# Low parts of the plain feed-forward weights by accumulating DMA, and the embeddings' projection kept in HBM during the feed-forward

## The chip, the cores and the metric

The kernel runs on one core of a Trainium2 chip. The time is the device time of one execution in microseconds, the median of three runs. The engines are TensorE (PE; its weight loads are shown as PEld), VectorE (DVE), ScalarE (ACT), GpSimd (POOL) and SyncE (SP). Each takes its instructions in the order of its own queue. SP only issues DMAs here; POOL issues others and computes a few small things.

## The reference

One layer of a hybrid encoder on 512 tokens of width 1024, in float32. Only the last two of its three parts matter here:

```python
x = x + jnp.concatenate([a, r], axis=-1) @ w_o[l]          # attention and recurrence, before
h = rms_norm(x, g_ffn[l])
x = x + (jax.nn.silu(h @ w_gate[l]) * (h @ w_up[l])) @ w_down[l]
gate = jax.nn.sigmoid(rms_norm(x, g_ple[l]) @ w_ple_gate[l])
x = x + gate * (p[l].astype(x.dtype) @ w_ple_proj[l])
```

`w_gate` and `w_up` have 1024 rows and 2816 columns, 22 tiles of 128 columns; `p @ w_ple_proj` is the projection of the embeddings, 1024 features by 512 tokens, eight tiles of 128 x 512.

## The kernel before

All activations lie with the features on the 128 partitions and the 512 tokens along the row. To keep precision at TensorE's fast float32 format, each operand is split in two: a rounded high part, and a low part that is the rest. A product is three matmuls (`mm3`, lines 141 to 144): high times high, high times low, low times high. `split` (lines 132 to 139) makes the parts: ScalarE copies the operand into the rounding format, VectorE subtracts.

A second way to make a low part is there already for other weights (lines 154 to 157, 1160 to 1170): the high part is scaled by -1 into the low tile by ScalarE, and a DMA issued by POOL adds the same weights from HBM onto it (`accum_op=ALU.add`).

The feed-forward works on 22 pairs (a tile of `w_gate` and the same tile of `w_up`), in six parts of 4, 4, 4, 4, 3 and 3. After each part, eight products with `w_down` (names `dn`) add the part to the residual `xT`. The pairs of part 0 are plain (`pair_plain`, line 1036): `halves` (line 1019) loads the weight in two halves of 512 columns (tiles `raw`, `whi`, `wlo`), and 24 matmuls make one 128 x 512 result (`ff`). The result is multiplied by the token scale `bc2`. That scale comes from `token_rstd` (line 179) after the second plain tile: sums by TensorE (`ss`), VectorE, a power of -1/2 by POOL (`rs_tok`), eight small VectorE instructions (`dgh`, `dgl`), and two matmuls (`bc`, lines 195 and 196) that spread it over the partitions. TensorE's order puts these two matmuls behind the third plain tile.

The pairs of the other parts use seven half-size products in place of eight (`pair_seven`, line 1096): weights A11, A21, A22, A12 are loaded raw (line 1102, tiles `A`), VectorE makes sums of them (`S`, line 1112), each of the seven operands is split, and meets sums of the activations, which `block_sums` (line 1074) makes once, beside the plain pairs. These products are named `p`.

The embeddings' projection is made before the feed-forward, at the end of the mixer (lines 944 to 955): its eight results are copied by ScalarE to tiles `ppo`, and stay in SBUF until the last stage (lines 1232 to 1250), where each multiplies the gate.

Tiles of 128 x 512 come from a list of places, `A` (class `Slots`): `get` takes the first free place, `put` puts it at the end. A place is given out in program order, but the instruction that writes it waits on the chip until the last reader of the tile before has finished. A longer list of free places means that a place has lain longer when it comes around again. The order on each engine is made by a scheduler that works from a timeline of its own, so a change in places changes the order too.

Of the kernel before, what the change touches and what calls it, by code (L numbers as in the profile page):

```python
# [8 lines left out]
F32 = mybir.dt.float32  # L9
F32R = mybir.dt.float32r  # L10
I32 = mybir.dt.int32
AF = mybir.ActivationFunctionType
ALU = mybir.AluOpType
AX = mybir.AxisListType

P = 128
S = 512
NT = S // P
KT = 8
# [98 lines left out]
def layer_kernel(ctx: ExitStack, tc: tile.TileContext, io, out):  # L118
    nc = tc.nc
    act, dve, pool, pe, sp = nc.scalar, nc.vector, nc.gpsimd, nc.tensor, nc.sync  # L120

    cpool = ctx.enter_context(tc.tile_pool(name="cpool", bufs=1))
    small = ctx.enter_context(tc.tile_pool(name="small", bufs=4))
    spool = ctx.enter_context(tc.tile_pool(name="spool", bufs=1))
    ppool = ctx.enter_context(tc.tile_pool(name="ppool", bufs=1, space=bass.MemoryType.PSUM))
    mixer = ExitStack()
    wpool = mixer.enter_context(tc.tile_pool(name="wpool", bufs=WB))
    A = Slots(spool, SLOTS, "u")
# [3 lines left out]
    def split(hi, lo, src, scale=None, eng=dve):  # L132

        if scale is None:
            act.activation(hi, src, AF.Copy)  # L135
            eng.tensor_tensor(lo, src, hi, ALU.subtract)  # L136
        else:
            act.activation(hi, src, AF.Copy, scale=scale)
            dve.scalar_tensor_tensor(lo, src, scale, hi, ALU.mult, ALU.subtract)
# [24 lines left out]
    def cut(hl, a, b):  # L164
        return hl[0][:, a:b], hl[1][:, a:b]

    def ts(j):
        return slice(j * P, (j + 1) * P)

    def rsqrt_mean(o, ss, n):  # L170

        w = ss.shape[-1]
        v = small.tile([P, 8], F32, tag="rs_v", name="rs_v")
        dve.tensor_scalar(v[:, :w], ss, 1.0 / n, EPS, ALU.mult, ALU.add)
        pool.tensor_tensor(o, v[:, :w], mhalf[:, :w], ALU.pow)
# [3 lines left out]
    def token_rstd(sq, keep=None):  # L179


        p1 = B.get("ss")
        for j in range(NT):
            e = pe.matmul(p1[:, j : j + 1], lhsT=sq[:, ts(j)], rhs=ones[:, :1], start=True, stop=True)
        rs = (keep or small).tile([P, NT], F32, tag="rs_tok", name="rs_tok")
        rsqrt_mean(rs, p1[:, :NT], 1024.0)
        B.put(p1)

        dh, dl = A.get("dgh", F32R), A.get("dgl", F32R)
        for j in range(NT):  # L190
            dve.tensor_scalar(dh[:, ts(j)], ident, rs[:, j : j + 1], None, ALU.mult)
            dve.scalar_tensor_tensor(dl[:, ts(j)], ident, rs[:, j : j + 1], dh[:, ts(j)], ALU.mult, ALU.subtract)
        marks.append(e.ins)
        p2 = B.get("bc")
        pe.matmul(p2, lhsT=onesr, rhs=dh, start=True, stop=False)
        marks.append(pe.matmul(p2, lhsT=onesr, rhs=dl, start=False, stop=True).ins)
        bc = A.get("rsbc")
        act.copy(bc, p2)
        A.put(dh, dl)
        B.put(p2)  # L200
        return rs, bc
# [34 lines left out]
    t = B.get("warm")  # L236
# [365 lines left out]
    def wnext():  # L602
        while wlist and len(ahead) < AHEAD:
            nd[0] += 1
            ahead.append(weights(*wlist.popleft(), by_dma=nd[0] > LO_DVE))
        return ahead.popleft()
# [14 lines left out]
    def w_in_tokens(evacuate):  # L621

        for half in range(2):
            ws = [wnext(), wnext()]
            for jp in range(2):
                o = [BD.get("wt0"), BD.get("wt1")]
                for c in range(2):
                    for k in range(4 * c, 4 * c + 4):
                        a = (k % 4) * 256
                        for i in range(2):  # L630
                            j = 2 * jp + i
                            mm3(o[i][:, :256], cut(hT[k], j * P, j * P + P), cut(ws[c], a, a + 256), k == 0, k == KT - 1)
                        if k % 2:
                            yield 1.3
                for i in range(2):
                    evacuate(2 * jp + i, slice(half * 256, half * 256 + 256), o[i][:, :256])
                BD.put(*o)

    def gates(heads):

        zs = {}
        for h in heads:
            for d in range(2):
                z = []
                yield from w_in_tile(z)
                zs[h, d] = z[0]
        for h in heads:
            z = []
            yield from w_in_tile(z)
            q[h] = z[0]  # L650

        later.append(gate_steps(heads, zs))
# [3 lines left out]
    def spread(stream):  # L656

        for y in stream:
            yield y
            if later and next(later[0], None) is None:  # L660
                later.popleft()
# [35 lines left out]
    def output_gates():  # L697

        zs = []
        for h in range(H):  # L700
            yield from w_in_tile(zs)
        t = [A.get("sg") for h in range(H)]
        together([lambda h=h: act.activation(t[h], zs[h], AF.Sigmoid) for h in reversed(range(H))], exp_ln)
        for h in range(H):
            dve.scalar_tensor_tensor(zs[h], zs[h], vec[:, V_HGO + h : V_HGO + h + 1], t[h], ALU.mult, ALU.mult)
        A.put(*t)
        gg.extend(zs)
# [202 lines left out]
    def load_embeddings():  # L910
        for k in range(2):
            t = A.get("pin")
            sp.dma_start(t, io["pT"][k])
            hl = (A.get("ph", F32R), A.get("pl", F32R))
            split(hl[0], hl[1], t)
            A.put(t)
            pT.append(hl)

    def dense_stream():
        for what in ORDER:  # L920
            if what == "v":
                yield from spread(w_in_tokens(value_out))
                done.add("value")
            elif what == "g":
                yield from spread(output_gates())
            elif what == "p":
                load_embeddings()
            else:
                yield from spread(gates(what))
        done.add("gate")  # L930
        while later:
            if next(later[0], None) is None:
                later.popleft()
        for hl in hT:
            A.put(*hl)
        A.put(bc1)
        for m in range(KT):
            xT[m] = A.get(f"x{m}")
            sp.dma_start(xT[m], io["xT"][m])
        yield lambda: "attention" in done  # L940
        yield from w_o_half(0, aT, BD)
        for h in range(H):
            A.put(*aT[h])
        for c in range(2):
            w = wnext()
            for i in range(4):
                o = BD.get("pp")
                for k in range(2):
                    a = (i * 2 + k) * P
                    mm3(o, cut(w, a, a + P), pT[k], k == 0, k == 1)  # L950
                t = A.get("ppo")
                act.copy(t, o)
                BD.put(o)
                pp.append(t)
                yield 1.3
        for hl in pT:
            A.put(*hl)

    pp = []
# [56 lines left out]

    A.join(Slots(ctx.enter_context(tc.tile_pool(name="fpool", bufs=1)), SLOTS2, "f"), 12)

    def halves(src):

        ws = []
        for i in range(2):
            raw, hi, lo = A.get("raw"), A.get("whi", F32R), A.get("wlo", F32R)
            sp.dma_start(raw, src[:, i * 512 : i * 512 + 512])
            split(hi, lo, raw)
            A.put(raw)
            ws.append((hi, lo))
        return ws

    def part_of(ws, k):  # L1030
        return cut(ws[k // 4], k % 4 * P, k % 4 * P + P)

    bc2 = None
    tiles_done = 0

    def pair_plain(f):

        nonlocal bc2, tiles_done
        zz = []
        for name in ("w_gate", "w_up"):  # L1040
            w = halves(io[name][f])
            o = B.get("ff")
            with ExitStack() as behind:

                if tiles_done > 1:
                    behind.enter_context(tc.issue_after(marks[-4 + min(tiles_done, 3)]))
                for k in range(KT):
                    mm3(o, part_of(w, k), h2[k], k == 0, k == KT - 1)
            A.put(*w[0], *w[1])
            tiles_done += 1  # L1050
            if bc2 is None:
                bc2 = token_rstd(sq2)[1]
                A.put(sq2)
            z = A.get("z")
            dve.tensor_tensor(z, o, bc2, ALU.mult)
            B.put(o)
            zz.append(z)
        hl = (A.get("ah", F32R), A.get("al", F32R))
        act.activation(zz[0], zz[0], AF.Silu)
        dve.tensor_tensor(zz[0], zz[0], zz[1], ALU.mult)  # L1060
        split(hl[0], hl[1], zz[0])
        A.put(*zz)
        return hl
# [126 lines left out]
    f = 0  # L1190
# [38 lines left out]
        next_down()  # L1229


    rs3, bc3 = token_rstd(sq3)
    for m in range(KT):
        w = halves(io["w_pg"][m])
# [92 lines left out]
```

## Time and profile before

| | |
|---|---|
| median of three runs | 702.74 us (701.41 to 702.83) |
| the profiled execution | 700.41 us, of which the span of the trace is 698.6 |
| TensorE busy | 686.4 us (98%) |
| VectorE, ScalarE, POOL busy | 509.5, 383.2, 111.1 us (73, 55, 16%) |
| feed-forward | from 295 to 648 us: plain pairs to 348, seven-product pairs among the `dn` products after that; then the last stage |
| HBM read, written | 88.33 MB, 2.10 MB |

Times in rows are microseconds from the span's start. A row of the timeline is one instruction (or several merged, with their count behind the x): start, duration, engine, line, operation, the tiles it writes and reads, and in brackets how long the engine stood idle before it and what ended that. A busy TensorE is not TensorE at its peak: ends of matmuls are modelled, and the distance between two starts says more.

### The profile page before, as it was taken

Reading aid. Unit: us, or ns where it says so; the run is one execution under the profiler, and the core shown is the slowest. Engines: PE = TensorE matmul, PEld = TensorE weight load, DVE = VectorE, ACT = ScalarE, POOL = GpSimd, SP = SyncE. Lnnn points to the kernel's source line nnn. Section 1 sums busy time; section 2 is a strip of 40 time slices with the busy share of each in tenths; the row PEclk is TensorE's granted clock in tenths of the full one; section 3 lists DMA queues with packets and bytes.
Section 4 is the critical chain, followed back from the end, with each engine's and each line's share of the span. In section 5 each row is a group of like instructions: output and inputs, shape, how many; then the busy total and the mean of one; then the engine's idle time right before and its main releaser. Section 6 shows DMA issues by size and latency. Waiting matters only on the chain.

```text
span 698.6 us, 11350 instructions
## 1 busy us (share of the span) xinstructions
PE 686.4 (98%) x4170; PEld 604.2 (86%) x4170; DVE 509.5 (73%) x1031; ACT 383.2 (55%) x808; POOL 111.1 (16%) x144
## 2 busy tenths in 40 slices
PE   9999999899999999999989999999999999999997
PEld 8888887699878888878788999999999999998886
DVE  6944489797987943679987977877677578768663
ACT  7857795686645645535544554445544545546421
POOL 6233421101212222010111100001100110100000
PEclk9999999999999999999999999999999999999999
DMA  7575555543657657322456456345655664563111
GB/s 241 164 171 136 124 145 97 119 86 84 157 123 208 156 138 189 90 66 61 147 129 163 115 145 178 92 115 145 166 130 130 158 138 123 123 179 112 55 60 61
DMA packets 44264, 91.18 MB, mean 131 GB/s; under 512 B 5424, under 2 KB 11568, under 8 KB 44208
## 3 DMA queue, kind: packets, MB, share of 16 engines
q0 software_dynamic: 14976, 41.43, 28.8%
q1 hardware_dynamic: 29232, 49.02, 22.3%
q8 instruction: 33, 0.54, 0.3%
q14 instruction: 23, 0.19, 0.1%
HBM read 88.33 MB, written 2.10 MB: 129 GB/s over the span
## 4 chain that ended last, share of the span: by engine, by line
PE 86%; issue 8%; DMA 2%; ACT 2%; POOL 1%; DVE 1%; SPq 0%; POOLq 0%; ACTq 0%
PE p L144 8%; PE p L143 8%; PE p L142 8%; PE dn L143 5%; PE dn L144 5%; PE dn L142 5%; PE wi L143 4%; PE wi L142 4%; PE wi L144 4%; PE pg L144 2%; PE pg L142 2%; PE pg L143 2%; PE wo L142 2%; PE wo L144 2%; PE wo L143 2%
## 5 line engine op out<-in xcount | busy, mean ns | idle before, releaser
L142 PE MATMUL p<-bh,whi 128*128 128x256 f32 x432 | 122.3, 284 | 2.4 <-ACT whi L135 2.3
L143 PE MATMUL p<-bl,whi 128*128 128x256 f32 x432 | 121.8, 283 | 0.0
L144 PE MATMUL p<-bh,wlo 128*128 128x256 f32 x432 | 121.3, 283 | 0.0
L142 PEld LDWEIGHTS p<-bh,whi 128*128 128x128 f32 x432 | 82.7, 192 | 3.3 <-ACT whi L135 3.2
L143 PEld LDWEIGHTS p<-bl,whi 128*128 128x128 f32 x432 | 82.8, 192 | 0.1
L144 PEld LDWEIGHTS p<-bh,wlo 128*128 128x128 f32 x432 | 82.5, 192 | 0.1
L143 PE MATMUL dn<-al,whi 128*128 128x512 f32 x176 | 68.7, 390 | 0.0
L144 PE MATMUL dn<-ah,wlo 128*128 128x512 f32 x176 | 68.5, 389 | 0.0
L142 PE MATMUL dn<-ah,whi 128*128 128x512 f32 x176 | 67.7, 390 | 0.0
L1170 POOL DMA_DIRECT2D wlo<-in_w_d x32 | 27.4, 877 | 202.4 <-ACT wlo L1169 160.5
L1112 DVE TENSOR_TENSOR S<-A,A 128x512 f32<-128x512 f32 x36 | 24.4, 689 | 40.0 <-DMA A<-in_w_up 19.5
L135 ACT ACTIVATE whi<-A 128x512 fp32r<-128x512 f32 x54 | 33.6, 626 | 35.0 <-DMA A<-in_w_gate 22.8
L142 PE MATMUL wi<-hh,whi 128*128 128x512 f32 x128 | 51.2, 400 | 0.0
L144 PE MATMUL wi<-hh,wlo 128*128 128x512 f32 x128 | 50.9, 397 | 0.0
L143 PE MATMUL wi<-hl,whi 128*128 128x512 f32 x128 | 50.5, 394 | 0.0
L135 ACT ACTIVATE whi<-S 128x512 fp32r<-128x512 f32 x72 | 42.6, 623 | 10.3 <-DVE S L1112 9.0
L156 ACT ACTIVATE wlo<-whi 128x1024 fp32r<-128x1024 f32 x28 | 29.7, 1060 | 33.4 <-DMA whi<-in_w_hf 12.0
L136 DVE TENSOR_TENSOR wlo<-S,whi 128x512 fp32r<-128x512 f32 x72 | 46.3, 681 | 1.0 <-ACT whi L135 1.0
L135 ACT ACTIVATE whi<-raw 128x512 fp32r<-128x512 f32 (+2 forms) x42 | 25.5, 625 | 31.6 <-DMA raw<-in_w_up 9.7
L136 DVE TENSOR_TENSOR wlo<-A,whi 128x512 fp32r<-128x512 f32 x54 | 36.8, 682 | 3.1 <-ACT whi L135 3.1
L144 PEld LDWEIGHTS dn<-ah,wlo 128*128 128x128 f32 x176 | 33.1, 188 | 6.9
L142 PEld LDWEIGHTS dn<-ah,whi 128*128 128x128 f32 x176 | 33.0, 188 | 6.4
(342 smaller groups left out, 1840.6 us busy)
## 6 DMA issues: line engine op xcount, KB each, us to landing
A<-in_w_gate SPq DMA_DIRECT2D x36, 256.0 KB, 4.4
A<-in_w_up SPq DMA_DIRECT2D x36, 256.0 KB, 3.8
wlo<-in_w_d POOLq DMA_DIRECT2D x32, 256.0 KB, 5.3
whi<-in_w_hf POOLq DMA_DIRECT2D x14, 512.0 KB, 4.6
wlo<-in_w_hf POOLq DMA_DIRECT2D x14, 512.0 KB, 5.7
raw<-in_w_d SPq DMA_DIRECT2D x24, 256.0 KB, 2.8
x<-in_xT SPq DMA_DIRECT2D x16, 256.0 KB, 4.4
raw<-in_w_pg SPq DMA_DIRECT2D x16, 256.0 KB, 3.5
```

The costliest lines, as they stand in the source:

```text
L135: act.activation(hi, src, AF.Copy)
L136: eng.tensor_tensor(lo, src, hi, ALU.subtract)
L142: pe.matmul(o, lhsT=l[0], rhs=r[0], start=start, stop=False)
L143: pe.matmul(o, lhsT=l[0], rhs=r[1], start=False, stop=False)
L144: pe.matmul(o, lhsT=l[1], rhs=r[0], start=False, stop=stop)
L156: act.activation(lo[:, :cols], hi[:, :cols].bitcast(F32), AF.Copy, scale=-1.0)
L1112: dve.tensor_tensor(r[n], r[a], r[b], op)
L1170: pool.dma_start(lo[:, n], src, accum_op=ALU.add)
```

## The change

In the plain pairs after the first (`tiles_done > 1`: twelve of the sixteen halves), the low part is no longer subtracted by VectorE: ScalarE scales the raw weights by -1 into `wlo`, and a DMA from POOL adds the weights from HBM onto it. The eight results of the embeddings' projection are written to HBM by SP as they are made, their places are put back on the list, and after the feed-forward SP loads them again (tiles `ppi`).

```diff
@@ -122,6 +122,7 @@
+    dpool = ctx.enter_context(tc.tile_pool(name="dpool", bufs=1, space=bass.MemoryType.DRAM))
@@ -951,7 +952,10 @@
                 t = A.get("ppo")
                 act.copy(t, o)
                 BD.put(o)
-                pp.append(t)
+                kept = dpool.tile([P, S], F32, tag=f"pp{len(pp)}", name=f"pp{len(pp)}")
+                sp.dma_start(kept, t)
+                A.put(t)
+                pp.append(kept)
                 yield 1.3
@@ -1016,13 +1020,18 @@
-    def halves(src):
+    def halves(src, by_dma=False):
 
         ws = []
         for i in range(2):
             raw, hi, lo = A.get("raw"), A.get("whi", F32R), A.get("wlo", F32R)
             sp.dma_start(raw, src[:, i * 512 : i * 512 + 512])
-            split(hi, lo, raw)
+            if by_dma:
+                act.activation(hi, raw, AF.Copy)
+                act.activation(lo, raw, AF.Copy, scale=-1.0)
+                pool.dma_start(lo, src[:, i * 512 : i * 512 + 512], accum_op=ALU.add)
+            else:
+                split(hi, lo, raw)
             A.put(raw)
             ws.append((hi, lo))
         return ws
@@ -1038,7 +1047,7 @@
         for name in ("w_gate", "w_up"):
-            w = halves(io[name][f])
+            w = halves(io[name][f], tiles_done > 1)
@@ -1229,6 +1238,10 @@
         next_down()
 
 
+    for m in range(KT):
+        t = A.get("ppi")
+        sp.dma_start(t, pp[m])
+        pp[m] = t
     rs3, bc3 = token_rstd(sq3)
     for m in range(KT):
         w = halves(io["w_pg"][m])
```

Line numbers of the changed kernel are one higher from line 126 on, four higher from 956 on and nine higher from 1036 to 1231. Three places show how the order moves.

SP's loads around the start of the feed-forward, in the kernel before. The raw tiles are, from the top: first half of the third pair's `w_gate`, second half of the first `w_up`, first half of the second `w_gate`, both halves of the third `w_up`, second half of the last `w_gate`, both halves of the last `w_up`; then A11, A22, A21 of the first seven-product pair and A11 of the second.

```order
L1024 DMA raw_3588<-in_w_gate 128x512
L1024 DMA raw_3410<-in_w_up 128x512
L1024 DMA raw_3475<-in_w_gate 128x512
L1024 DMA raw_3627<-in_w_up 128x512
L1024 DMA raw_3633<-in_w_up 128x512
L1024 DMA raw_3709<-in_w_gate 128x512
L1024 DMA raw_3742<-in_w_up 128x512
L1024 DMA raw_3748<-in_w_up 128x512
L1102 DMA A_507_3811<-in_w_gate 128x512
L1102 DMA A_509_3815<-in_w_up 128x512
L1102 DMA A_508_3813<-in_w_up 128x512
L1102 DMA A_538_3997<-in_w_gate 128x512
```

The same place in the changed kernel: second half of the third `w_gate`, both halves of the third `w_up`, second half of the first `w_up`, first half of the second `w_gate`, A11 and A21, then first half of the third `w_gate`, both halves of the last `w_up`, A22 and A12.

```order
L1028 DMA raw_3617<-in_w_gate 128x512
L1028 DMA raw_3651<-in_w_up 128x512
L1028 DMA raw_3658<-in_w_up 128x512
L1028 DMA raw_3428<-in_w_up 128x512
L1028 DMA raw_3493<-in_w_gate 128x512
L1111 DMA A_507_3841<-in_w_gate 128x512
L1111 DMA A_508_3843<-in_w_up 128x512
L1028 DMA raw_3610<-in_w_gate 128x512
L1028 DMA raw_3770<-in_w_up 128x512
L1028 DMA raw_3777<-in_w_up 128x512
L1111 DMA A_509_3845<-in_w_up 128x512
L1111 DMA A_510_3847<-in_w_gate 128x512
```

The weights of the first seven-product pair have moved up into the plain pairs' loads, two of them ahead of the first half of the third `w_gate`.

POOL's queue around the token scale (`rs_tok`), in the kernel before; the DMAs beside it are weights of `w_down`.

```order
L157 DMA wlo_3166<-in_w_or 128x1024
L1160 DMA whi_3583<-in_w_d 128x512
L1162 DMA wlo_3584<-in_w_d 128x512
L175 TENSOR_TENSOR rs_tok<-rs_v,mhalf 128x4
L1160 DMA whi_3698<-in_w_d 128x512
L1162 DMA wlo_3699<-in_w_d 128x512
```

The same place in the changed kernel, from behind the last DMA of `w_o` on (the row `wlo_3184` ahead of these); the new ones are those of L1032, and `wlo_3612` is the first half of the third `w_gate`.

```order
L1032 DMA wlo_3543<-in_w_up 128x512
L1032 DMA wlo_3502<-in_w_gate 128x512
L1032 DMA wlo_3619<-in_w_gate 128x512
L1169 DMA whi_3605<-in_w_d 128x512
L1032 DMA wlo_3653<-in_w_up 128x512
L1032 DMA wlo_3660<-in_w_up 128x512
L1032 DMA wlo_3495<-in_w_gate 128x512
L1171 DMA wlo_3606<-in_w_d 128x512
L1032 DMA wlo_3612<-in_w_gate 128x512
L176 TENSOR_TENSOR rs_tok<-rs_v,mhalf 128x4
L1032 DMA wlo_3738<-in_w_gate 128x512
```

Seven new accumulations and the two DMAs of `w_down` now stand between the last weight of `w_o` and the token scale; one more new accumulation stands ahead of them.

ScalarE at the start of the feed-forward, in the kernel before: the normalized inputs (`hh`) and their squares come in pairs, and `whi_3405` is the high part of the first half of the first `w_up`.

```order
L138 ACTIVATE hh_3305<-x_310_2592,vec 128x512
L209 ACTIVATE sq_3309<-x_310_2592 128x512
L138 ACTIVATE hh_3313<-x_311_2594,vec 128x512
L209 ACTIVATE sq_3317<-x_311_2594 128x512
L135 ACTIVATE whi_3405<-raw_3404 128x512
L1161 ACTIVATE wlo_3584<-whi_3583 128x512
```

The same place in the changed kernel, where `whi_3423` is that high part. A copy for `whi_3618`, the second half of the third `w_gate`, stands further up, behind the first of the eight pairs of normalized input and square.

```order
L139 ACTIVATE hh_3323<-x_310_2594,vec 128x512
L210 ACTIVATE sq_3327<-x_310_2594 128x512
L1031 ACTIVATE wlo_3619<-raw_3617 128x512
L139 ACTIVATE hh_3331<-x_311_2596,vec 128x512
L210 ACTIVATE sq_3335<-x_311_2596 128x512
L136 ACTIVATE whi_3423<-raw_3422 128x512
L139 ACTIVATE hh_3339<-x_312_2598,vec 128x512
```

Two copies, `whi_3618` and `wlo_3619`, now stand ahead of `whi_3423` among the same six pairs.

## Rows read from the trace of the kernel before

**Rows 1.** Stretches: length, busy us (instructions) of PE, PEld, DVE, ACT, POOL, clock, DMA, GB/s.
```profile
314.60:345.50 30.90, 30.51 (x139) 24.90 (x138) 30.79 (x59) 17.93 (x31) 2.34 (x4) 1.00 0.31 88
345.50:356.00 10.50, 8.12 (x47) 6.43 (x46) 8.71 (x16) 5.84 (x11) 2.28 (x3) 1.00 0.83 218
...
390.00:648.00 258.00, 258.00 (x1742) 239.73 (x1741) 195.85 (x340) 132.72 (x256) 27.39 (x32) 1.00 0.54 138
```

**Rows 2.** Timeline of TensorE in the first two plain tiles.
```profile
298.12 0.63 PE L142 MATMUL ff<-hh,whi 128*128 128x512 f32 x2
298.59 0.40 PE L143 MATMUL ff<-hl,whi 128*128 128x512 f32 x1
299.39 0.50 PE L143 MATMUL ff<-hl,whi 128*128 128x512 f32 x1 [0.40 <-DVE hl L139]
...
300.66 0.39 PE L142 MATMUL ff<-hh,whi 128*128 128x512 f32 x1
301.26 0.50 PE L144 MATMUL ff<-hh,wlo 128*128 128x512 f32 x1 [0.21 <-DVE wlo L136]
```

**Rows 3.** Timeline of TensorE from the last plain tile into the seven-product pairs.
```profile
339.31 0.39 PE L144 MATMUL dn<-ah,wlo 128*128 128x512 f32 x1
339.83 0.39 PE L142 MATMUL p<-b11h,whi 128*128 128x256 f32 x1
...
343.14 0.39 PE L143 MATMUL ff<-hl,whi 128*128 128x512 f32 x1
343.79 0.39 PE L144 MATMUL p<-b11h,wlo 128*128 128x256 f32 x1 [0.26 <-DVE wlo L136]
...
348.65 0.28 PE L143 MATMUL p<-b11l,whi 128*128 128x256 f32 x1
350.04 0.39 PE L142 MATMUL p<-bh,whi 128*128 128x256 f32 x1 [1.11 <-ACT whi L135]
...
353.81 0.28 PE L143 MATMUL p<-bl,whi 128*128 128x256 f32 x1
353.94 0.28 PE L144 MATMUL p<-bh,wlo 128*128 128x256 f32 x1
355.45 0.39 PE L142 MATMUL p<-bh,whi 128*128 128x256 f32 x1 [1.24 <-ACT whi L135]
```

**Rows 4.** Timeline of ScalarE, copies that waited for loads.
```profile
309.89 0.63 ACT L135 ACTIVATE whi<-raw 128x512 fp32r<-128x512 f32 x1 [7.43 <-DMA raw<-in_w_up]
...
349.36 0.63 ACT L135 ACTIVATE whi<-A 128x512 fp32r<-128x512 f32 x1 [0.98 <-DMA A<-in_w_gate]
...
354.77 0.63 ACT L135 ACTIVATE whi<-A 128x512 fp32r<-128x512 f32 x1 [3.22 <-DMA A<-in_w_gate]
```

**Rows 5.** Tiles `raw` from 295 to 345 us: count, ns min/median/max, starts.
```profile
L136 DVE TENSOR_TENSOR wlo<-raw,whi x11: 678/681/693, 299.9 to 344.3; 128x512 fp32r<-128x512 f32 x11
```

**Rows 6.** Timeline of ScalarE, two copies behind each other in the first plain tiles.
```profile
297.49 0.62 ACT L135 ACTIVATE whi<-raw 128x512 fp32r<-128x512 f32 x1
298.01 0.62 ACT L1161 ACTIVATE wlo<-whi 128x512 fp32r<-128x512 f32 x1
```

**Rows 7.** Line 1162, eight accumulating DMAs of 256 KB from POOL.
```profile
DMA to landing us min/median/max: 3.9/4.2/7.3
```

**Rows 8.** Line 157, 28 accumulating DMAs of 512 KB from POOL.
```profile
DMA to landing us min/median/max: 5.1/5.6/8.8
```

**Rows 9.** Timeline of POOL around the token scale.
```profile
308.99 1.04 POOL L175 TENSOR_TENSOR rs_tok<-rs_v,mhalf 128x4 f32<-128x4 f32 x1 [9.20 <-DVE rs_v L174]
...
318.91 0.87 POOL L1162 DMA_DIRECT2D wlo<-in_w_d  x1 [3.94 <-ACT wlo L1161]
```

**Rows 10.** Timeline of VectorE, the last scalings behind the token scale.
```profile
310.85 1.14 DVE L192 SCALAR_TENSOR_TENSOR dgl<-cst,rs_tok,dgh 128x128 fp32r<-128x128 f32 x4
```

**Rows 11.** Timeline of TensorE, the first of the two scale matmuls.
```profile
314.12 0.39 PE L195 MATMUL bc<-dgh,onesr 128*128 128x512 f32 x1
```

**Rows 12.** Busy time by stretch, while the fifth part's places are free.
```profile
632.00:640.00 8.00, 8.00 (x37) 6.60 (x37) 6.10 (x12) 3.32 (x7) 0.00 (x0) 1.00 0.16 51
```

## The prediction, made before the changed kernel ran

> **What bounds the kernel now.** I read the page's busy shares first, where the reader sees TensorE at 98%: only a stretch in which it stands still can give anything back. Next comes the busy time by stretch of the feed-forward [rows 1]. From 390 to 648 us it is 258.00 of 258.00: nothing can be gained there, however early data comes. The losses lie before: 0.4 us while VectorE is full (30.79 of 30.90 from 314.6 to 345.5), 2.4 from 345.5 to 356, and some in the first tiles ahead of these. The granted clock is 1.00 throughout, the higher of its two levels, so the clock is no cause.
>
> Idle time understates a stop, because the last matmul's end is drawn out. I therefore take starts: 128x512 matmuls follow each other by 0.23 us (two of them from 298.12 to 298.59), 128x256 ones by 0.12 to 0.13 (353.81 to 353.94) [rows 2, 3]. By starts the early stops are 299.39 - 298.59 - 0.23 = 0.57 and 301.26 - 300.66 - 0.23 = 0.37, together 0.9 us [rows 2], both ended by VectorE. At the first seven-product pairs they are 343.79 - 343.14 - 0.23 = 0.42, 350.04 - 348.65 - 0.12 = 1.27 and 355.45 - 353.94 - 0.12 = 1.39, together 3.1 us [rows 3]. Smaller irregular starts up to 384, of which 339.83 - 339.31 - 0.23 = 0.29 is the first [rows 3], add, I estimate from the same pitch, 1.2 us. So 5.2 us stand to be won at most; the rest of the feed-forward already runs through.
>
> Who ends the two long stops? ScalarE's copy of an operand, and that copy itself waited 0.98 and 3.22 us for a load of w_gate [rows 4]. Those loads go into tiles that come free late: A12 of the first pair takes the place of the fourth scratch tile of block sums 2, which VectorE frees at about 345.5.
>
> **The change part by part.**
>
> Eight embedding tiles leave SBUF. Their places go to seven weight tiles and a result of the second plain pair, and whatever follows on the list gets a place that has lain longer. A11 and A21 of the first seven-product pair now follow the raw tiles of the third pair's w_up, which ScalarE has read by about 302; A22 and A12 follow that tile's high and low parts, which TensorE has read half through it, about 328; the second pair's four follow normalized inputs, which TensorE reads last in the last plain tile, from about 340 on. A load lands some 3 to 4 us later, so A12's copy stands at about 336 instead of 349.36 and the second pair's at about 345 instead of 354.77. TensorE, without the stops, reaches these products at about 347 and 352. The two long stops go: 2.7 us.
>
> Twelve subtractions leave VectorE, 0.68 us each; 9 of the 11 that it does between 295 and 345 are among them [rows 5]. Six of these fall after 314.6, in the full stretch: 6 x 0.6 (their pitch) = 3.6 us of an engine without slack, which ends the 0.42 stop and most of the irregular starts. What is late next there is VectorE still: the low parts of the first pair's operands, which I count at 340 to 346 for products from 345 on. I leave 0.2 us as residue.
>
> ScalarE gets twelve more copies, 0.52 us apart [rows 6]. Where it has idle time they cost nothing. They do cost in front of the high part of the first w_up tile's first half: in the order two copies of later weights stand ahead of it, among the same six pairs of normalized input and square. That operand started at 297.49 [rows 6] and TensorE took it at about 298.36, one matmul ahead of 298.59 [rows 2]; two more copies make it 298.5 to 299.1, a stop of 1.0 us, plus 0.2 for the low part behind it on VectorE. It takes the place of the 0.9 of rows 2, which then lie in its shade. Bounds: 0.5, if the normalized inputs are late as well, and 3.0, if the load for the first of these copies lands 2 us late, since all eight normalized inputs stand behind it on ScalarE.
>
> Twelve accumulating DMAs join POOL's queue, 0.9 us of issue each. Such a transfer of 256 KB lands 3.9 to 7.3 us after its issue, median 4.2 [rows 7]. Ten of the twelve have 5 us or more to spare by my count. Two have not. The second w_gate tile's first low part is scaled at about 304.5, issued at 305.1, landed at 309.3; TensorE wants it at 308.9: 0.4 us (0.1 to 3.5 by the bounds of rows 7). The last w_gate tile's first low part is issued at about 335.0, landed at 339.2, wanted at 339.9: nothing (to 2.4).
>
> Behind POOL's first new DMA stands the last load of w_o. It also waits for the last embedding matmul, which now stands some 2 us later. Its low part then is issued at about 280.7 and lands, by the 5.6 us of such 512 KB transfers [rows 8], at 286.3, wanted at 286.0: 0.3 us (0 to 3.5).
>
> The Trainium skill bears on these terms. "DMA: Bandwidth & Descriptors", section "Anatomy of one DMA — SWDGE (gpsimd) path", fits a DMA issued from GpSimd as 2.0 us plus its bytes over 436 GB/s, an estimate of 2.6 us for 256 KB. By it the low parts counted at 0.4 and 0.3 us would be in time, and the sum 0.7 us better; rows 7 show no such transfer under 3.9 us, so I keep 4.2. "SBUF — State Buffer", section "SBUF: two separate sides", speaks against the change: GpSimd cannot write descriptors while VectorE is in a two-port mode. By it a DMA issued under a full VectorE would land about 2.5 us later, an estimate from its 620 against 3100 ns, and the second w_gate tile would cost 2.9 instead of 0.4. In the trace the accumulation at 318.91 was issued in 0.87 us in the stretch where VectorE was full [rows 1, 9], and among the eight of rows 7 its 4.0 us to landing is no slow one.
>
> The embeddings' way out and back is 16 DMAs of 256 KB on SP. The writes stand between 257 and 274 in front of weight loads that in the kernel before were issued at about the same time, since both wait for the same copies; I take 0 (to 1). On the way back eight loads stand in SP's queue after the ninth load of w_pg. Their tiles are the fifth part's activations and last weights, free when its last product ends, about 632, and from 632 to 640 the DMA engines are 16% busy [rows 12]. The first tile is wanted at about 673. Cost 0; if the tiles came free only with the other w_pg loads, at 640, eight times some 0.75 us would shift these by 6 us, into a stage where they have about as much to spare.
>
> Sum against the profiled execution, 700.41 us (span 698.6 and 1.8 around it): won 0.9 + 3.1 + 1.2 = 5.2; paid 1.0 + 0.2 + 0.4 + 0.3 + 0.2 = 2.1; net 3.1, so 697.3. The median of the runs is 2.3 us above this execution, so 702.74 - 3.1 = 699.6.
>
> **The rivals.**
>
> *A: the root of the token sums is held up in POOL's queue (slower).* It stands behind eight accumulations there. In the trace it runs from 308.99 for 1.04 us [rows 9], VectorE's eight scalings take until 312.0 [rows 10], and TensorE asks at 314.12 [rows 11]: 2.1 us to spare. The last of the eight waits for the third w_gate tile's first load, which stands in SP's queue behind A11 and A21, and these wait for ScalarE. I count that load's landing at 306.3, the accumulation's issue at 307.6, the root at 308.8. It decides from a landing at about 308.5; from there each microsecond costs one, since all work of the stage needs this scale. If the load came as late as one of the third w_up did before, for which ScalarE waited 7.43 us [rows 4], it would land at 313.7, 5.2 us past that point: 699.6 + 5.2 = 704.8. For it: the long queue. Against: its tile is a scratch tile that is free by 303.
>
> *B: the stop changes hands (no difference).* Loads come early, but low parts from a full VectorE take over at the first pairs: the 3.1 us of rows 3 stay, 699.6 + 3.1 = 702.7. For it: 30.79 of 30.90. Against: the two long stops name loads, and 3.6 us leave VectorE.
>
> *C: all cover holds.* No new stop at all, only the ScalarE order costs its 0.5: 702.74 - 5.2 + 0.5 = 698.0.
>
> *D: the accumulations are late throughout.* Each of the three close ones takes its upper bound, 3.5 + 2.4 + 3.5 instead of 0.7, 8.7 us more: 708.3; half of that, 704.
>
> **How the numbers follow.** My forecast, with its own range of 698 to 701, has 0.45; C 0.17; B 0.20; A 0.08; D 0.10. Differences of 0.2% (1.4 us) are about what a measurement of this kernel can tell from none. Forecast and C are faster by more, and I take 0.02 of B with them: 0.64. B gives 0.18 to no difference, and D's mild half 0.03: 0.21. Slower: A and the rest of D, 0.15. The range goes from 697.0, below C by what irregular starts I may have undercounted, to 703.8, which takes in B and leaves A and most of D out.
>
> **What would show it.** Right: in the profile after, TensorE's waits for ScalarE's operands at the first seven-product pairs gone, and its busy time from there to the last stage equal to the stretch; w_gate and w_up loads of the first pair issued before 330; POOL's root starting before 311; one stop of about 1 us some 3 us into the first plain tile. Wrong: a stop on a low part in a plain tile of more than 1 us with an accumulation as its releaser, a late scale matmul (A), a wait for w_pg or the embeddings in the last stage, or stops of the old size with VectorE as releaser (B).

## The result and the profile after

The changed kernel is slower: 724.67 us (720.16 to 726.40, four runs) against 702.60 us for the kernel before on the same chip, a ratio of 1.031 (1.028 to 1.034). The forecast was 699.6 with a range of 697.0 to 703.8. The profiled execution took 720.16 us, 19.8 more than that of before; it is the fastest of the four, so what its trace shows is a little less than the loss of the median, 22.1.

The shares of the chain that ended last, by engine, from the page of the kernel before and from that of the changed one; transfers (DMA) went from 2% to 11%:

```profile
PE 86%; issue 8%; DMA 2%; ACT 2%; POOL 1%; DVE 1%; SPq 0%; POOLq 0%; ACTq 0%
```

```profile
PE 66%; issue 12%; DMA 11%; DVE 6%; ACT 3%; POOL 2%; SPq 1%; POOLq 0%; DVEq 0%; ACTq 0%
```

The changed kernel's busy time by stretch (columns as in [rows 1]):

```profile
240.00:300.00 60.00, 55.00 (x350) 45.22 (x350) 19.80 (x46) 23.47 (x59) 12.39 (x15) 0.97 0.69 175
300.00:325.00 25.00, 22.08 (x99) 17.11 (x98) 17.06 (x33) 17.26 (x31) 7.17 (x9) 1.00 0.67 150
325.00:378.00 53.00, 53.00 (x310) 47.03 (x309) 45.26 (x85) 31.03 (x58) 10.36 (x15) 1.00 0.57 139
378.00:530.00 152.00, 151.53 (x1048) 141.73 (x1047) 115.51 (x199) 74.10 (x143) 17.34 (x21) 1.00 0.52 128
530.00:660.00 130.00, 122.04 (x778) 110.35 (x777) 90.44 (x158) 60.34 (x122) 12.97 (x15) 0.97 0.55 147
```

The stretch that was to be won is won: where TensorE had lacked 2.4 us [rows 1], it now runs 53.00 of 53.00. But it stands still ahead of it, and from 530 on, where the kernel before had 258.00 of 258.00. TensorE's five largest groups of waits from 260 to 660 us (sum, times, longest):

```profile
PE dn L143 <- ACT ah L136: 5.2, 1, 5.2
PE rT L865 <- DVE r L861: 3.5, 1, 3.5
PE ff L145 <- DMA wlo<-in_w_gate: 2.4, 1, 2.4
PE p L145 <- DVE wlo L137: 1.7, 2, 1.5
PE rT L865 <- ACT r L859: 1.3, 1, 1.3
```

Measured as in the prediction, from start to start less the pitch of each shape (summed where positive), TensorE lost in each profiled execution (us):

| kernel | to 240 | 240-300 | 300-325 | 325-400 | 400-700 |
|---|---|---|---|---|---|
| before | 28.0 | 9.6 | 1.5 | 5.3 | 1.2 |
| changed | 29.8 | 16.1 | 4.7 | 0.9 | 13.6 |
| e1 embeddings through HBM only | 29.6 | 15.6 | 2.8 | 8.0 | 22.7 |
| e2 accumulating DMAs only | 29.3 | 11.1 | 2.1 | 2.3 | 1.2 |
| e3 places held | 29.2 | 17.1 | 2.3 | 3.1 | 1.2 |
| e4 places joined later | 30.1 | 19.8 | 2.4 | 1.2 | 17.8 |
| e5 places, no traffic | 31.0 | 14.7 | 7.1 | 1.1 | 9.0 |
| e6 late writes | 29.1 | 11.0 | 9.7 | 3.5 | 10.7 |
| e7 late writes, own places | 30.0 | 11.3 | 11.6 | 5.6 | 1.3 |
| e8 DMAs, own places | 27.4 | 12.7 | 1.6 | 3.1 | 1.3 |
| e9 changed, own places | 29.8 | 15.7 | 7.3 | 1.8 | 1.5 |
| e10 four places held | 30.2 | 19.6 | 1.2 | 6.7 | 5.7 |
| e11 spread writes, own places | 28.9 | 13.7 | 2.8 | 7.1 | 1.2 |
| e12 as e8, last `w_up` by VectorE | 29.7 | 10.2 | 1.5 | 1.9 | 1.4 |

The change cost 6.5 us at the mixer's end, 3.2 in the first plain tiles and 12.4 late; it gained 4.4. (The columns are cut by time: about 0.9 us of the first plain tile, its stop at 299.39 [rows 2] among it, stand ahead of 300 in the kernel before and behind 300 in the changed one. Cut at the first `ff` product, the mixer's end lost 7.4 and the first tiles 2.3.) Up to 240 the instructions stand as before on every engine, and that column varies by 3.6 from run to run.

**The mixer's end.** DMAs issued from 260 to 290 us (line, engine, count, size, median us to landing), first of the kernel before, then of the changed one:

```profile
whi<-in_w_or POOLq DMA_DIRECT2D x2, 512.0 KB, 6.4
```

```profile
pp<-ppo SPq DMA_DIRECT2D x7, 256.0 KB, 6.2
...
whi<-in_w_or POOLq DMA_DIRECT2D x2, 512.0 KB, 8.1
```

Beside the writes of the embeddings on SP's queue the loads of `w_o` on POOL's take 8.1 instead of 6.4 us. The Trainium skill states this, in "DMA: Bandwidth & Descriptors", section "Issuing engines are not separate DMA queues": transfers issued by different engines run on the same 16 DMA engines and interleave. The trace agrees, by these 1.7 us (two loads each), and by the same difference in the experiments below: 8.6 us in e3, which has the writes, against 6.9 in e2, which has none (three loads each). ScalarE, TensorE and VectorE at this place:

```profile
272.01 1.06 ACT L157 ACTIVATE wlo<-whi 128x1024 fp32r<-128x1024 f32 x1 [4.76 <-DMA whi<-in_w_or]
...
285.94 0.63 ACT L1030 ACTIVATE whi<-raw 128x512 fp32r<-128x512 f32 x1 [7.62 <-DMA raw<-in_w_up]
...
288.16 0.37 ACT L859 ACTIVATE r<-po,ro 128x128 f32<-128x128 f32 x1 [0.32 <-DVE r L861]
```

```profile
284.38 0.39 PE L145 MATMUL wo<-rTh,wlo 128*128 128x512 f32 x1
288.27 0.30 PE L865 MATMUL rT<-cst,r 128*128 128x128 f32 x1 [3.51 <-DVE r L861]
```

```profile
287.17 0.69 DVE L137 TENSOR_TENSOR wlo<-raw,whi 128x512 fp32r<-128x512 f32 x1 [8.78 <-ACT whi L136]
287.78 0.34 DVE L861 TENSOR_SCALAR r<-po,ro 128x128 f32<-128x128 f32 x1
```

The last results of the recurrence (`r`) were ready to be scaled at about 279.5, when POOL's root of their sums was done. But in the order three copies of feed-forward weights stand ahead of them on ScalarE, and a subtraction that needs the second copy on VectorE. ScalarE sat 7.62 us in front of the first copy, VectorE 8.78 in front of the subtraction. TensorE waited for `r`. Why that load came late is on SP's queue:

```profile
270.82 0.33 SPq L1028 DMA_DIRECT2D raw<-in_w_up  x1
273.56 2.32 SPq L956 DMA_DIRECT2D pp<-ppo  x3
280.12 0.33 SPq L1028 DMA_DIRECT2D raw<-in_w_up  x1
280.54 0.98 SPq L1028 DMA_DIRECT2D raw<-in_w_gate  x2
```

The `w_up` load issued at 280.12, of the second pair, takes the place of an embedding whose write landed at 280.06; the two `w_gate` loads, for the very first tile and so wanted earlier, stand behind it. SP's waits of this kind from 270 to 281 us:

```profile
SPq L1028 <- DMA pp<-ppo: 10.4, 2, 6.2
```

**The late stops.** SP's queue before the last pair, and its longest wait from 598 to 626 us:

```profile
602.36 0.38 SPq L1111 DMA_DIRECT2D A<-in_w_gate  x1
616.99 0.33 SPq L1111 DMA_DIRECT2D A<-in_w_up  x1
...
623.30 0.33 SPq L1111 DMA_DIRECT2D A<-in_w_gate  x1
626.91 8.11 SPq L1174 DMA_DIRECT2D raw<-in_w_d  x8
635.11 7.52 SPq L1028 DMA_DIRECT2D raw<-in_w_pg  x6
```

```profile
SPq L1111 <- DVE u L1147: 14.2, 1, 14.2
```

For 14.2 us SP issued nothing: the last pair's A22 has the place of `u2` of two pairs before, a scratch tile with which a pair's products are added up. Its last reader ran on VectorE just ahead of the load:

```profile
616.24 0.69 DVE L1147 TENSOR_TENSOR u<-p,u 128x512 f32<-128x512 f32 x1
```

Behind this load stood three more loads of this pair, eight of `w_down` and then those of `w_pg`. In the kernel before the four loads of this pair were issued from 590.5 to 600.1, 16 to 25 us ahead of its first product at 615.84; here from 617.0 to 623.3, 5 to 11 us ahead of it at 627.86. What was squeezed behind them met ScalarE:

```profile
644.22 1.57 ACT L136 ACTIVATE whi<-raw 128x512 fp32r<-128x512 f32 x3 [2.65 <-DMA raw<-in_w_pg]
647.50 2.08 ACT L136 ACTIVATE whi<-raw 128x512 fp32r<-128x512 f32 x4 [1.71 <-DMA raw<-in_w_pg]
649.49 0.40 ACT L1153 ACTIVATE u<-u 128x256 f32<-128x256 f32 x1
...
651.68 0.63 ACT L136 ACTIVATE ah<-e 128x512 fp32r<-128x512 f32 x1 [0.23 <-DVE e L1154]
```

```profile
646.80 0.39 PE L143 MATMUL dn<-ah,whi 128*128 128x512 f32 x1
652.37 1.22 PE L143 MATMUL dn<-ah,whi 128*128 128x512 f32 x2 [5.18 <-ACT ah L136]
653.39 0.63 PE L144 MATMUL dn<-al,whi 128*128 128x512 f32 x1
653.82 0.63 PE L145 MATMUL dn<-ah,wlo 128*128 128x512 f32 x1
```

The last activation (`u` at 649.49, then `ah`) stands on ScalarE behind high parts of `w_pg`, whose loads are late; the sum that it needs (`u`, line 1149) ran on VectorE only at 647.31, behind low parts that wait for such copies. From the end of the last pair's products to `ah` it took 13.7 us (651.68 - 637.94), before 6.4 (632.28 - 625.91), while the products that TensorE has in between last 8.9 us.

### The profile page after: what moved, and what is told of

It reads as the page before. It is cut to its first block, busy times and chain, and to the rows that moved or that the text cites. A ratio compares the mean times of both kernels' runs of the same rounds, so it can differ in the third digit from the quotient of the medians.

```text
span 718.4 us, 11424 instructions
## 1 busy us (share of the span) xinstructions
PE 692.9 (96%) x4170; PEld 608.5 (85%) x4170; DVE 502.3 (70%) x1019; ACT 387.6 (54%) x820; POOL 120.6 (17%) x156
## 4 chain that ended last, share of the span: by engine, by line
PE 66%; issue 12%; DMA 11%; DVE 6%; ACT 3%; POOL 2%; SPq 1%; POOLq 0%; DVEq 0%; ACTq 0%
PE p L145 7%; PE p L143 7%; PE p L144 7%; PE dn L143 4%; PE dn L144 4%; PE dn L145 4%; PE wi L145 3%; PE wi L144 3%; PE wi L143 3%; DVE wlo L137 2%; PE pg L144 2%; PE pg L143 2%; PE pg L145 2%; DMA raw<-in_w_d 2%; PE ff L145 2%
## 5 line engine op out<-in xcount | busy, mean ns | idle before, releaser
L143 PE MATMUL dn<-ah,whi 128*128 128x512 f32 x176 | 69.6, 400 | 5.7 <-ACT ah L136 5.2
L157 ACT ACTIVATE wlo<-whi 128x1024 fp32r<-128x1024 f32 x28 | 29.7, 1060 | 34.9 <-DMA whi<-in_w_hf 12.0
L1121 DVE TENSOR_TENSOR S<-A,A 128x512 f32<-128x512 f32 x36 | 24.5, 686 | 24.9 <-DMA A<-in_w_up 17.8
L144 PEld LDWEIGHTS dn<-al,whi 128*128 128x128 f32 x176 | 33.7, 192 | 6.8 <-DVE al L137 0.5
```

The costliest lines, as they stand in the source:

```text
L143: pe.matmul(o, lhsT=l[0], rhs=r[0], start=start, stop=False)
L144: pe.matmul(o, lhsT=l[0], rhs=r[1], start=False, stop=False)
L157: act.activation(lo[:, :cols], hi[:, :cols].bitcast(F32), AF.Copy, scale=-1.0)
L1121: dve.tensor_tensor(r[n], r[a], r[b], op)
```

## The experiments

Each is timed against the kernel before on its chip: 701.74 us for e1 to e4, 702.34 for e5 to e8, 702.17 for e9 to e11, 701.82 for e12. The first four split the change and its places.

**e1.** The changed kernel without the accumulating DMAs:

```
-            w = halves(io[name][f], tiles_done > 1)
+            w = halves(io[name][f])
```

> Only the embeddings' way through HBM; the low parts of the plain pairs are made by VectorE as before. By summed starts TensorE lost, against the kernel before, 9.6 us more between 260 and 300, 3.0 between 300 and 320, 4.7 between 540 and 616 and 7.7 from 640 on (4.2 less at 340 to 356). Theory (places): the first feed-forward loads take the embeddings' places, wait in SP's queue for the writes to land, and ScalarE's copies of these loads stand ahead of the last scalings of the recurrence's results; so this kernel keeps the stops at 272 and 284, loses the 2.5 us at 318, and keeps the late ones: 716 to 721. Rival (accumulations): the twelve new DMAs on POOL's queue and their copies on ScalarE are the cause; then this one stands near 700 to 706.

731.23 us (1.038 to 1.046). The embeddings' way alone costs more than the whole change; the size was beyond both forecasts. The stops at 272 and 284 (1.8 and 2.9 us) and a late one of 5.9 are there, the stop at 318 is not. The accumulating DMAs are worth 6.6 us in this company (731.23 - 724.67; 7.4 if each is counted from the kernel before on its chip).

**e2.** The changed kernel with the embeddings kept in SBUF (and the loading back left out):

```
...
-                sp.dma_start(kept, t)
-                A.put(t)
-                pp.append(kept)
+                pp.append(t)
...
```

> Only the accumulating DMAs; the embeddings stay in SBUF. Theory (places): no stop at 272 or 284 and none in the fifth part, a stop of 0.5 to 2.5 us on a low part in the second w_gate tile: 702 to 706. Rival (accumulations): 713 or more, with the stops of 3.7 and 5.3 us.

701.35 us (0.997 to 1.001): no difference, and no late stop. The rival (accumulations) falls.

**e3.** The changed kernel without giving the places back:

```
                 sp.dma_start(kept, t)
-                A.put(t)
                 pp.append(kept)
```

> As the changed kernel, with the writes and the reading back, but the embeddings' eight SBUF places are never given to anything else, so no load waits for a write. Theory (places): the stops at 272 and 284 go, and as the places are then as many as before, the late stops too: 702 to 708. Rival (transfers): the sixteen transfers of 256 KB delay the loads around them by themselves; then 714 to 724 and the stops stay.

709.53 us (1.008 to 1.016), between the two forecasts. Both were half right. With the sixteen transfers, but the list of before, nothing is lost from 400 on; so the reading back is free. The mixer's end stays as bad (17.1), though no load waits for a write: there the writes cost 6 us against e2 by themselves.

**e4.** The places are collected in `held`, and joined behind those that the feed-forward opens:

```
+    A.put(*held)
```

> As the changed kernel, but the eight places join the free list only behind the places that the feed-forward opens, so they are taken late, long after their writes have landed. Theory (places): the stops at 272 and 284 go. If the late stops come with the delay of the mixer, the time is 701 to 707; if they come with the longer list of places in the seven-product stage, they stay and it is 711 to 717. Rival (transfers): 718 to 724.

726.49 us (1.033 to 1.039): above every range, the rival's too: a miss. The late stops stay (17.8), as the list is as long as in the changed kernel, and the mixer's end is worse (19.8), though the places are taken late; why it is worse than in the changed kernel (16.1) is not shown.

**e5.** The changed kernel without the writes, the loads back and the multiplication by them:

```
-                sp.dma_start(kept, t)
                 A.put(t)
...
-        sp.dma_start(t, pp[m])
...
-            dve.tensor_tensor(z[:, c], z[:, c], pp[m][:, c], ALU.mult)
```

> As the changed kernel, but the embeddings are neither written nor read: their tiles go back to the list as soon as they are made, and the last stage leaves out the multiplication by them (eight VectorE instructions of the tail, less than 1 us). So eight more places and no added traffic on SP's queue. Theory (which tile had a load's place before): in the list of places the loads of the seven-product pairs then follow the scratch tiles that a pair frees at its end (25 of 72 loads, against 3 in the kernel before, where 16 follow activations that a part has long freed), so the late stops (4.7 us between 540 and 616, 7.7 from 640 on) stay without any added transfer: 708 to 717. Rival (traffic: the reading back among the w_pg loads makes the stop at 647): 697 to 703.

717.97 us (1.021 to 1.028), 1 us above the theory's range. The twelve accumulating DMAs are still there, which cost nothing in e2; eight more places without the embeddings' sixteen transfers cost 15.6 us against the kernel before, of which 7.8 are late. So the rival falls. (Counted again, 21 of the 72 loads follow `u2`, `u34`, `e` or `S4`, against 2 before.) SP's wait ahead of the last pair and TensorE's waits after 390 are those of the changed kernel:

```profile
SPq L1108 <- DVE u L1144: 13.2, 1, 13.2
```

```profile
PE dn L143 <- ACT ah L136: 2.7, 1, 2.7
PE p L145 <- DVE wlo L137: 2.6, 3, 1.7
```

**e6.** The writes and the giving back stand behind the loads of the first pair (`loads[3]` is its last):

```
+                if i == 0:
+                    with tc.issue_after(loads[3]):
+                        for m, t in enumerate(pp):
...
+                            sp.dma_start(pp[m], t)
+                            A.put(t)
```

> As the changed kernel, but the eight writes are queued on SP behind the loads of the first feed-forward tile, and the places are given back there. Theory: in the mixer's last 40 us nothing is added, so the stops at 272 and 284 are those of the kernel with the accumulating DMAs alone (1.2 and 1.1); the late stops stay, since the list of places is as long as in the changed kernel: 710 to 717. Rival (the late stops follow from a mixer that ends late): 697 to 704.

717.97 us (1.020 to 1.028), 1 us above the range. The mixer's end is that of e2 (11.0, 11.1), so 5 of the 6.5 us lost there come from the writes and places; the other 1.5 are there without them too. The late stops stay (10.7) behind a mixer that is on time: the rival falls. New is 9.7 in the first tiles, where eight writes in one piece now stand ahead of loads.

**e7.** e6, and a list of eight places for A11, A21, A22, A12:

```
+        if part == 1:
+            ring = A.part("R", 8)
...
-            r[n] = A.get(n)
+            r[n] = ring.get(n)
...
-        A.put(r["A21"])
+        ring.put(r["A21"])
```

> As the run with late writes, but the first-stage loads of the seven-product pairs (A11, A21, A22, A12) take turns on eight places of their own, so each follows a load of two pairs before, which the operands' splits free early; all else has the list of places less eight. Theory (which tile had the place before): the late stops go, 697 to 702. Rival (too many places or too early an order of loads by themselves): the loads of w_d or w_pg are late in their place and it stays above 706.

710.04 us (1.006 to 1.017). The late stops are gone (1.3), as expected; the time is 8 us above the theory's range, and the first tiles, where the writes are, lost 10.1 us more than before (11.6).

**e8.** e2 with the same eight places (`ring = A.part("R", 8)` and its `get` and `put`, as in e7).

> The accumulating DMAs, the embeddings kept in SBUF, and the eight places of their own for the seven-product loads. Theory: no late stops, and the first seven-product loads still follow tiles freed at 345, so about 701, no different from the accumulating DMAs alone (699 to 704). Rival: taking eight places out of a list that is short already delays the loads of w_d: 705 to 712.

701.30 us (0.996 to 1.000): as expected.

**e9.** The changed kernel with the same edit as e8 (`r[n] = ring.get(n)`), nothing else.

> The changed kernel with one difference: the loads A11, A21, A22 and A12 of the seven-product pairs take turns on eight places of their own. Theory: by summed starts the changed kernel loses 12.4 us from 540 to 660 that the kernel before does not; these go, the losses up to 340 stay: 724.7 - 12.4 = 712, 709 to 715. Rival (the late stops come from the late mixer, or from the reading back of the embeddings): 720 to 726.

709.82 us (1.007 to 1.015), 14.9 less than the changed kernel (12.4 expected). Between the two profiled executions it is 9.4: 12.1 us fewer are lost from 400 on, and 2.6 more in the first tiles. TensorE from 530 on:

```profile
530.00:625.00 95.00, 95.00 (x651) 88.68 (x650) 68.90 (x118) 48.64 (x97) 13.48 (x16) 1.00 0.57 144
625.00:665.00 40.00, 40.00 (x217) 34.85 (x217) 32.17 (x56) 22.26 (x41) 0.00 (x0) 1.00 0.44 135
```

With the same mixer (15.7), the same traffic and as many places, the late stops go when the loads follow loads instead of scratch. The rival falls.

**e10.** Every second embedding's place is given back:

```
+                if len(pp) % 2:
                     A.put(t)
```

> The changed kernel, but only four of the embeddings' eight places go back to the list, so the list is four longer than before. Of the 72 loads of the seven-product pairs 10 then follow scratch that a pair frees at its end (3 in the kernel before, 25 in the changed one). Theory (which tile had the place): late stops of 2 to 6 us, between none and 12.4; with the writes' cost in the mixer 711 to 718. Rival (any added place is enough): the late stops of the changed kernel in full, 720 or more.

717.56 us (1.017 to 1.027), late losses 5.7: 4.5 above before, as the theory had it (nine loads behind such scratch, counted again). The mixer's end (19.6) is worse than with all eight places, which is not explained.

**e11.** e7 with each write behind a load of its own:

```
+                with tc.issue_after(loads[3]), tc.issue_after(at):
+                    sp.dma_start(pp[m], t)
+                    A.put(t)
```

> The kernel with late writes and the eight places, but the eight writes stand singly or in pieces behind the loads of the second to fourth feed-forward tiles, so that no load that is wanted within 10 us stands behind them. Theory: no stops in the mixer, none after 390, and the 3.7 us twice at 312 and 317 of the run with the writes in one piece go: 698 to 703. Rival (writes delay the loads of this stretch wherever they stand): 705 to 711.

704.64 us (1.002 to 1.007). The stops at 312 and 317 go, but one of 4.2 us for a low part of `w_up` comes at 352: missed, between the two forecasts. Six of the eight writes still stood in one piece.

**e12.** e8 with `1 < tiles_done < 7` as the condition:

> As the run with the accumulating DMAs, the embeddings in SBUF and the eight places of their own, but the last w_up tile of the plain pairs is split by VectorE again: there TensorE waited 1.4 us for an accumulating DMA. Theory: that wait goes, VectorE has the 1.4 us to spare behind the last full stretch: 700 (698 to 702). Rival (VectorE is full up to 345, so its two subtractions are late by as much): no different, 701 to 703.

700.11 us, ratio 0.9973 (0.9953 to 0.9993): the only version whose interval lies below the kernel before, by 1.7 us. The wait for an accumulating DMA that it was to remove (1.4 us in e8) is gone from its trace. Its middle and its feed-forward:

```profile
325.00:378.00 53.00, 51.68 (x319) 46.56 (x319) 51.74 (x97) 29.89 (x56) 5.66 (x8) 1.00 0.57 152
390.00:648.00 258.00, 258.00 (x1732) 239.39 (x1731) 193.41 (x329) 132.07 (x253) 27.07 (x32) 1.00 0.53 133
```

Which of its parts (the accumulating DMAs, the eight places, the last `w_up` tile back on VectorE) brings the 1.7 us was not separated; the times of e8 and e12 were taken on different chips.

## Why the prediction was wrong

**The step that failed: "whatever follows on the list gets a place that has lain longer" (the section on the kernel before has it too). It cost 12.4 us from 400 on, where I had forecast nothing.** That is so in program order, and not in time. The list is refilled in program order, but loads run a pair or more ahead of products. A place given back by a pair's own load is free early, since VectorE and ScalarE read loads well ahead of the products; one given back by the scratch of a pair before it (`u2`, `u34`, `e`) stands earlier in the program, but is free only when that pair's products are added up (616.24 for the place of the last pair's A22). In the kernel before most of the 72 loads followed weights, loads of the last pair and activations of a finished part; eight more places moved 21 of them onto scratch. e5 shows the late loss without the embeddings' traffic; with that traffic it goes when the list is short again (e3) or the loads have places of their own (e9), and with four added places it lies in between (e10). I read 258.00 of 258.00 [rows 1] as a stretch where nothing can be gained, and did not ask what it rested on.

**"The writes ... I take 0 (to 1)": 5.0 us of the 6.5 lost in the mixer's last 60 us.** I compared issue times and gave neither the eight loads' waits for the writes nor the 512 KB loads beside them a price. e6 shows that this loss leaves with the writes and places. How it divides is not settled: transfers alone (e3) and places alone (e5) lost 6.0 and 3.6 us more than e2, both together 5.0. The other 1.5 us are lost in e2 as well, where only the accumulating DMAs are new; the prediction had 0.3 there.

**Right: the size of the gain.** The three stops of [rows 3] went; 4.4 us came from 325 to 400, of 3.1 + 1.2 counted. Whether it divides as I had it, 2.7 of it by earlier loads, is not shown: e2, with the list of before, already gains 3.0, and its waits for ScalarE's operands (`p` on `whi`) are 0.6 us instead of 2.3; in e1, with the longer list alone, these waits are gone as well, but other stops make the stretch worse (8.0). Of the first pair's four loads two were issued only at 340, not before 330, in a stage that ran some 9 us late.

**The second `w_gate` tile's low part: forecast 0.4 (0.1 to 3.5), measured 2.5 at 318, inside the bounds.** The usual time of such a transfer was right [rows 7]; all twelve:

```profile
DMA to landing us min/median/max: 3.7/4.3/7.3
```

The mis-sized term is this one's landing:

```profile
314.80 0.86 POOL L1032 DMA_DIRECT2D wlo<-in_w_gate  x1 [1.82 <-ACT wlo L1031]
```

```profile
320.74 0.50 PE L145 MATMUL ff<-hh,wlo 128*128 128x512 f32 x1 [2.36 <-DMA wlo<-in_w_gate]
```

It was issued behind two accumulations for a later `w_up` tile and landed 5.9 us later, at 320.70, where I had taken the median of 4.2; the rest of the chain stands as I counted it, some 9 us later. The two accumulations ahead of it took 6.0 and 7.2 us, so three were under way at a time. VectorE was idle for most of this time (2.8 us ahead of 317.84 and 5.0 us behind it), so a full VectorE is not what held it up. e2, where the list is shorter and these loads come later, has no such stop.

**The last `w_o` load: forecast 0.3.** POOL issued it at 289.78 instead of 280.7, behind a wait of 10.3 us for `r`; TensorE itself waited for `r`, so it shows as no stop of its own.

**ScalarE's order: forecast 1.2, measured 0.9.** By starts the first plain tile lost 0.43 us at 307.39, for a low part of the inputs (`hl`), and 0.46 at 308.64, for the high part behind the two added copies: no more than the two early stops of [rows 2], which these took the place of.

**Reading back: forecast 0, right** (e3, e9 lose nothing there).

**Rival A met its condition and not its price.** The root of the token sums ran at 321.65, 13 us beyond my 308.8, and VectorE waited 5.0 us for it. Some 9 us of the 13 are no matter of the queue: the sums that it works on (`rs_v`) came at 317.84, in the kernel before at 308.74. The accumulations held it for the rest. POOL's timeline:

```profile
321.65 1.35 POOL L176 TENSOR_TENSOR rs_tok<-rs_v,mhalf 128x4 f32<-128x4 f32 x1
```

TensorE had plain products to do until 325.89, where the order now places the scale, and no stop followed. Rivals B, C and D did not come: the late stops lay where none of my cases looked.

**"Twelve subtractions leave VectorE":** with the embeddings in SBUF this is worth nothing measurable in the whole time (e2), with the embeddings away 6.6 us (e1 against the changed kernel).

## What to carry to other kernels

When a first-in first-out list of buffers changes length, look up for each load which tile had its place before, and when on the chip that tile's last reader runs; a longer list can hand loads the places of the latest tiles. Here it helped to give prefetched loads places of their own, taken by turns. Price a transfer put into a busy stretch by what stands behind it on its queue and by what runs beside it, not by its issue time.

## What the runs showed of the hardware

After the stops of 3.7 and 5.3 us TensorE ran at the lower of its two levels, 1.2 GHz instead of 2.4; after that of 2.5 us at 318 it did not. The granted clock (the column behind POOL's) behind the two stops:

```profile
288.30:292.00 3.70, 3.70 (x12) 2.89 (x13) 0.69 (x2) 1.95 (x4) 1.82 (x2) 0.54 0.18 19
652.30:657.00 4.70, 4.63 (x11) 3.67 (x12) 2.95 (x5) 0.01 (x1) 0.00 (x0) 0.50 0.47 170
```

Each 128x512 matmul started 0.43 instead of 0.23 us behind the last (653.82 - 653.39), and the eleven between 652.3 and 657 cost 2.4 us on top of the stop. So this stop of 5.3 us cost 7.7. The length of a stop alone does not tell what the clock does: in e3 a wait of 1.8 us for `r` at 273.60 was followed by the lower level (the mean of 260 to 280 us is 0.91), while the wait of 2.4 us at 318 was not (1.00 from 300 to 325).
